# A causal mask added by VectorE where it finds the row maximum, with three smaller moves, in a two-layer hybrid block

## The chip, the cores and the metric

The kernel runs on one core of one Trainium2 chip. The metric is the device time of one execution in microseconds (us); lower is better. Of the kernel before there are three timed runs, 1093.37, 1095.77 and 1095.83 us, with the median 1095.77. A further execution was recorded by the hardware profiler: its own time is 1094.5 us, and the span that the trace covers is 1092.8 us.

## The reference

A block of two layers works on 512 tokens of width 1024 in float32. Each layer mixes tokens, adds the normed result to the residual `h`, and runs a gated feed-forward network of hidden width 2816. Layer 0 mixes by a gate with a spatial matrix per group of 128 columns; layer 1 mixes by attention with a forget gate over 12 heads of 64 columns. Both layers also attend over 256 memory rows with 4 heads. What the change touches is this:

```
# layer 0: spatial gating; w is lower triangular, its rows are summed where ln_b enters
s = einsum('gts,bcsgd->bctgd', tril(w_s), layernorm(gelu(v), ln_g, ln_b)) + b_s
# layer 1: forgetting attention, per head
c = cumsum(log_sigmoid(s_in @ w_f + b_forget))              # the gate sums
logits = q k^T * scale + c[t] - c[s]
logits = where(s <= t, logits, -inf)
o = softmax(logits) @ v
# end of layer 1
h = h + rmsnorm(f, ln_ffn_post[1])                          # the last scale rows are ln_ffn_post[1]
```

## The kernel before

Every float32 product is made of three matmuls: a value is split into a high part (`whi`, a cast by ScalarE, line 276) and a low part (`wlo`, the rest, a subtraction by VectorE, line 277), and `mm3` multiplies high by high, low by high and high by low (lines 219 to 221). So every weight that arrives by DMA passes through ScalarE and VectorE before TensorE can use it. The feed-forward networks use a seven-product scheme for block pairs and take most of the time; the change touches them only at their edges.

A scheduler orders the work: it gives each engine and each DMA queue one fixed list, and a queue runs its list strictly in order. The order of the program text sets the priorities. Pools of buffers hold the scheduler to a number of live tiles: PSUM has three tags, `mm` and `lg` with three tiles each and `tr` with two.

The masked attention of layer 1 is run by `attend` (line 562), one head after the other, in steps. While head n gets its logits, the probabilities of head n-1 are turned and multiplied. `S3`, `S2`, `S1`, `S0` are `FoxHead.logits` (line 530) for blocks of 128 queries; block tb has (tb+1) x 128 keys, so 512, 384, 256 and 128 columns of `lg` in PSUM. `N` steps scale the probabilities `p` by the reciprocal of their sums `sm` (lines 478 and 480). `T` steps turn them by TensorE (line 487) and split the turned tile `tr` into the two parts `pT`; `V` steps multiply by the values (line 556). `F` steps take other work in between: here the value and key projections that are still to be done (`v`, `qk`), and later the first part of the output projection (`y`).

One call of `logits` issues two float32 matmuls for the head (`qa` with `ka`, then `qc` with `kc`, whose rows 64 to 67 carry the gate sums) and a third one in bfloat16, `ident_b` times `neg`, which adds the causal mask to the 128 columns on the diagonal (line 537). Then `weigh` (line 467) finds the negated maximum `nmx` by VectorE from PSUM (line 470), and ScalarE takes the exponent from PSUM into `p` with the sum of each row in `sm` (line 471).

The parts of a head, `qa`, `qc`, `ka` and `kc`, are put together by eight transfers on SP's queue in `head_parts` (lines 1567 to 1578): six copy parts of queries and keys, and two copy gate sums out of `cc`. `cc` is made from the `cs` matmuls (line 1546) by ScalarE and VectorE (lines 1550 to 1553). In the text, the first head's parts come behind `cc`.

The other three places: `spatial_bias` (line 735) sums the rows of the six triangular matrices with `tri`, in 12 matmuls of 128 columns (line 744); `boundary` (line 949) norms the residual between a mix and the product behind it, with `evacuate` called behind the second step (k = 1) of the third group of products, which puts the norm's factors into PSUM as `rb` (line 287) from `r`, a power taken by GpSimd (line 290); and `end_gains` (line 1619) turns the last scale rows into full tiles by eight TensorE transposes into `gr` (line 1625) and two copies by ScalarE (line 1628).

## Time and profile before

| what | value |
|---|---|
| timed runs, median (lowest to highest) | 1095.77 us (1093.37 to 1095.83) |
| the profiled execution, its own time | 1094.5 us |
| its span in the trace | 1092.8 us |
| mean granted TensorE clock | 0.998 |
| TensorE matmul busy | 99% |
| VectorE busy | 86% |
| ScalarE busy | 67% |
| GpSimd busy | 5% |
| mean DMA rate | 164 GB/s |

The difference of 1.7 us between the execution's own time and its span lies around the traced work. A matmul's row in the trace starts when it is taken up and includes the time through the array, so rows of neighbouring matmuls overlap; what one costs is read from the start of one to the start of the next. DVE is VectorE, ACT is ScalarE, POOL is GpSimd, PEld is TensorE's loading of weights, and SPq is SP's queue of DMA issues.

### The profile page before, as it was taken

What the parts mean: (1) busy time and instruction counts of PE and PEld (TensorE: products, weight loads), DVE (VectorE), ACT (ScalarE), POOL (GpSimd) and SP (SyncE); (2) the same over time, 40 slices, a digit from 0 to 9 for tenths busy, and PEclk for the clock granted to TensorE, in tenths of its full rate; (3) what the DMA queues carried; (4) which work ended last, traced back from release to release, by engine and by line L of the source; (5) the groups of instructions that cost most, each with busy time, mean ns of one, the idle gap of its engine ahead of it and who ended that gap; (6) DMA issues with size and microseconds to landing.
All of it is one profiled execution on the core that took longest, in us unless ns stands there. A gap on an engine that the chain in (4) does not pass through costs nothing.

```text
span 1092.8 us, 20047 instructions
## 1 busy us (share of the span) xinstructions
PE 1080.9 (99%) x7286; PEld 982.6 (90%) x7286; DVE 941.6 (86%) x1839; ACT 736.9 (67%) x1609; POOL 59.4 (5%) x74
## 2 busy tenths in 40 slices
PE   9999999999999999999999999999999999999997
PEld 7998889999999888998988888889999999988996
DVE  7889658999989999986987798958999998999975
ACT  8776458766666767567666577758766666667563
POOL 0101010000000000001110000010100000000000
PEclk9999999999999999999999999999999999999999
DMA  7554875867644447267592654535877553546232
GB/s 271 164 160 128 215 174 190 234 196 191 174 136 147 144 126 248 85 210 182 146 268 70 174 124 117 150 97 157 233 224 195 156 157 118 174 132 199 90 115 77
DMA packets 129834, 178.98 MB, mean 164 GB/s; under 512 B 8204, under 2 KB 92184, under 8 KB 129736
## 3 DMA queue, kind: packets, MB, share of 16 engines
q1 hardware_dynamic: 118376, 160.23, 46.8%
q0 software_dynamic: 10944, 17.30, 10.0%
q8 instruction: 57, 0.93, 0.3%
q14 instruction: 41, 0.34, 0.1%
q10 hardware_dynamic: 416, 0.18, 0.1%
HBM read 158.18 MB, written 42.99 MB: 184 GB/s over the span
## 4 chain that ended last, share of the span: by engine, by line
PE 89%; ACT 3%; DMA 3%; DVE 2%; issue 1%; POOL 1%; SPq 0%; POOLq 0%; DVEq 0%; ACTq 0%
PE a L219 7%; PE a L221 7%; PE a L220 7%; PE e L219 3%; PE e L220 3%; PE e L221 3%; PE ps L221 3%; PE ps L220 3%; PE ps L219 3%; PE y L219 3%; PE y L220 3%; PE y L221 3%; PE p L219 3%; PE p L221 3%; PE p L220 3%; PE x L219 3%
## 5 line engine op out<-in xcount | busy, mean ns | idle before, releaser
L277 DVE TENSOR_TENSOR wlo<-raw,whi 128x512 fp32r<-128x512 f32 x316 | 210.8, 685 | 21.4 <-ACT whi L276 18.2
L276 ACT CAST whi<-raw 128x512 fp32r<-128x512 f32 x316 | 189.0, 619 | 56.2 <-PE a L220 14.6
L219 PE MATMUL a<-xshi,whi 128*128 128x256 f32 x480 | 135.3, 282 | 0.0
L220 PE MATMUL a<-xslo,whi 128*128 128x256 f32 x480 | 134.7, 281 | 0.0
L221 PE MATMUL a<-xshi,wlo 128*128 128x256 f32 x480 | 134.5, 280 | 0.0
L276 ACT CAST whi<-room 128x512 fp32r<-128x512 f32 x160 | 98.3, 621 | 47.9 <-PE x L220 9.5
L277 DVE TENSOR_TENSOR wlo<-room,whi 128x512 fp32r<-128x512 f32 x160 | 108.7, 686 | 6.4 <-ACT whi L276 3.8
L219 PEld LDWEIGHTS a<-xshi,whi 128*128 128x128 f32 x480 | 90.4, 188 | 1.9 <-ACT e L1107 1.1
L220 PEld LDWEIGHTS a<-xslo,whi 128*128 128x128 f32 x480 | 90.4, 188 | 0.7
L221 PEld LDWEIGHTS a<-xshi,wlo 128*128 128x128 f32 x480 | 90.5, 188 | 0.0
L221 PE MATMUL ps<-xshi,wlo 128*128 128x256 f32 x192 | 54.3, 285 | 1.0 <-DVE wlo L277 1.0
L220 PE MATMUL ps<-xslo,whi 128*128 128x256 f32 x192 | 53.9, 283 | 0.6 <-DVE xslo L277 0.6
L219 PE MATMUL ps<-xshi,whi 128*128 128x256 f32 x192 | 53.7, 287 | 0.0
L276 ACT CAST ff<-u 128x256 fp32r<-128x256 f32 x80 | 32.3, 406 | 29.3 <-PE p L221 15.4
L219 PE MATMUL y<-whi,mixedhi 128*128 128x512 f32 x128 | 51.6, 403 | 0.0
L220 PE MATMUL y<-wlo,mixedhi 128*128 128x512 f32 x128 | 50.6, 395 | 0.0
L219 PE MATMUL p<-whi,ff 128*128 128x512 f32 x128 | 50.5, 396 | 0.0
L221 PE MATMUL y<-whi,mixedlo 128*128 128x512 f32 x128 | 50.5, 394 | 0.0
L220 PE MATMUL p<-wlo,ff 128*128 128x512 f32 x128 | 50.4, 394 | 0.0
L221 PE MATMUL p<-whi,ff 128*128 128x512 f32 x128 | 50.2, 394 | 0.0
L219 PE MATMUL x<-xshi,whi 128*128 128x256 f32 x160 | 45.0, 281 | 0.0
L220 PE MATMUL x<-xslo,whi 128*128 128x256 f32 x160 | 44.9, 281 | 0.0
(376 smaller groups left out, 3575.3 us busy)
## 6 DMA issues: line engine op xcount, KB each, us to landing
room<-in_w_up SPq DMA_DIRECT2D x36, 512.0 KB
raw<-in_w_gate SPq DMA_DIRECT2D x24, 512.0 KB
raw<-in_w_down SPq DMA_DIRECT2D x20, 512.0 KB
sums<-in_w_gate SPq DMA_DIRECT2D x16, 512.0 KB
sums<-in_w_gate POOLq DMA_DIRECT2D x16, 512.0 KB, 5.8
raw<-in_w_out SPq DMA_DIRECT2D x16, 512.0 KB
sums<-in_w_down SPq DMA_DIRECT2D x32, 256.0 KB
sums<-in_w_down POOLq DMA_DIRECT2D x16, 512.0 KB, 8.1
```

Of the source, the lines that this page charges most:

```text
L219: PE.matmul(o, w[0], x[0], start=start, stop=False, skip_group_check=more)
L220: PE.matmul(o, w[0], x[1], start=False, stop=False, skip_group_check=more)
L221: return PE.matmul(o, w[1], x[0], start=False, stop=stop, skip_group_check=more)
L276: last_hi[0] = A.copy(hi, src)
L277: last_split[0] = last_hi[0], (eng or V).tensor_sub(lo, src, hi)
```

## The change

Four parts move together.

1. The mask matmul is gone, and `ident_b` and `neg` with it. A constant `mask` (128 x 512 in bfloat16: zeros, and the triangle in the last 128 columns) takes their place. VectorE now makes one pass over `lg` that adds the mask, negates, writes the result to `p` in SBUF and keeps the least value, which goes to `nmx` by a second instruction. ScalarE takes the exponent in place, from `p` to `p`.
2. The last scale rows come by transfers: at the start of the program 1024 numbers of `gains` are written to a scratch tensor `row` in DRAM, and later two transfers spread its halves over 128 partitions.
3. `spatial_bias` takes two groups at a time: 6 matmuls of 256 columns.
4. The first head's parts stand ahead of the gate sums; only its two transfers from `cc` stay behind them. In `boundary`, `evacuate` is called one step of k later.

The diff, cut to its core:

```
-    ident_b = cp.tile([P, P], BF16, name="ident_b")
-    V.tensor_copy(ident_b, ident)
...
-    neg = cp.tile([P, P], BF16, name="neg")
-    V.tensor_copy(neg, neg_f[:, :P])
+    mask = cp.tile([P, T], BF16, name="mask")
+    V.tensor_copy(mask[:, : T - P], neg_f[:, P:])
+    V.tensor_copy(mask[:, T - P :], neg_f[:, :P])
...
-            PE.matmul(lg[:, :n], qc[:68, c], kc[:68, :n], start=False, stop=False)
-            PE.matmul(lg[:, c], ident_b, neg, start=False, stop=True)
+            PE.matmul(lg[:, :n], qc[:68, c], kc[:68, :n], start=False, stop=True)
...
-            self.weigh(tb, lg[:, :n], (self.beside if tb == 0 else self.room)[:, at : at + n])
+            p = (self.beside if tb == 0 else self.room)[:, at : at + n]
+            x = slice(tb, tb + 1)
+            V.tensor_tensor_reduce(out=p, in0=lg[:, :n], in1=mask[:, T - n :], scale=-1.0, scalar=3.0e38,
+                                   op0=ALU.add, op1=ALU.min, accum_out=self.nmx[:, x])
+            last_exp[0] = A.activation(p, p, AF.Exp, bias=self.nmx[:, x], scale=-1.0, accum_out=self.sm[:, x])
+            self.p[tb] = p
...
-                for n in range(2):
-                    o = ps("lg", (P, 384), s="rows")
-                    for g in range(3):
-                        for part in range(2):
-                            PE.matmul(o[:, g * P : (g + 1) * P], tri[:, 384:], ws[3 * n + g][:, part, :],
-                                      start=part == 0, stop=part == 1)
+                for n, both in enumerate(two_ws):
+                    o = ps("lg", (P, 2, P), s="rows")
+                    for part in range(2):
+                        PE.matmul(o, tri[:, 384:], both[:, :, part, :], start=part == 0, stop=part == 1)
...
-        outs = group(ws[:2], inputs(1), h0, ["mm", "lg"], after={1: evacuate})
+        outs = group(ws[:2], inputs(1), h0, ["mm", "lg"], after={2: evacuate})
...
+        def head_sums(u, n):
+            _, qc, _, kc = u.parts
+            nc.sync.dma_start(qc[66:68, :].bitcast(F32), cc[n : n + 33 : 32, :].bitcast(F32))
+            nc.sync.dma_start(kc[64:66, :].bitcast(F32), cc[64 + n : 64 + n + 33 : 32, :].bitcast(F32))
...
+            if n:
+                head_sums(u, n)
...
+        for f in before[-1]:
+            f()
         for f in take(fill, 2):
             f()
         cs = ps("mm", s="cs")
...
+        head_sums(heads[0], 0)
         ys, outs = out_part(1, mixed)
         more = queue(outs)
         credit[0] = 0
-        for f in take(fill, 2) + before[-1] + take(fill, 3):
+        for f in take(fill, 5):
...
+        row = dp.tile([KT, P], F32, tag="row", name="row")
+        c = (G_FFN_POST + 1) * KT
+        nc.sync.dma_start(row.rearrange("m c -> c m"), i["gains"][:, c : c + KT])
         for dh in range(2):
-            o = ps("tr", s="gr")
-            for m in range(4):
-                PE.transpose(o[:, m * P : (m + 1) * P],
-                             gain(G_FFN_POST + 1, 4 * dh + m).to_broadcast([P, P]), ident)
             gain_rows.append(plain("gr"))
-            A.copy(gain_rows[dh], o)
+            nc.sync.dma_start(gain_rows[dh], row[4 * dh : 4 * dh + 4, :].rearrange("m c -> (m c)").partition_broadcast(P))
```

How the lists move is shown at three places. First TensorE's list at the second head's first two blocks of logits (`lg` of 512 and 384 columns), with the turning of the first head's probabilities (`tr`) between them. Before:

```order
L535 MATMUL lg_7936<-ka_7829,qa_7828 128x512
L536 MATMUL lg_7936<-kc_7716,qc_7714 128x512
L537 LDWEIGHTS ident_b
L537 MATMUL lg_7936<-neg,ident_b 128x128
L487 MATMUL tr_7951<-ident,p_7862 128x128
L487 MATMUL tr_7951<-ident,p_7842 128x128
L487 MATMUL tr_7951<-ident,p_7825 128x128 x2
L535 MATMUL lg_7960<-ka_7829,qa_7828 128x384
L536 MATMUL lg_7960<-kc_7716,qc_7714 128x384
L537 LDWEIGHTS ident_b
L537 MATMUL lg_7960<-neg,ident_b 128x128
```

Now:

```order
L533 MATMUL lg_7926<-ka_7822,qa_7821 128x512
L534 MATMUL lg_7926<-kc_7657,qc_7655 128x512
L485 MATMUL tr_7940<-ident,p_7853 128x128
L485 MATMUL tr_7940<-ident,p_7834 128x128
L485 MATMUL tr_7940<-ident,p_7818 128x128 x2
L533 MATMUL lg_7949<-ka_7822,qa_7821 128x384
L534 MATMUL lg_7949<-kc_7657,qc_7655 128x384
```

The mask's matmul and its load of weights are gone after each block, and the rest keeps its order here.

VectorE's list at the same blocks (`nmx` is the negated maximum, `pT` the turned probabilities, `vf` values of a projection, `sm` the row sums). Before:

```order
L277 TENSOR_TENSOR pT_7929<-tr_7927,pT_7928 128x512
L470 TENSOR_REDUCE nmx_7723<-lg_7936 128x1
L277 TENSOR_TENSOR pT_7953<-tr_7951,pT_7952 128x512
L470 TENSOR_REDUCE nmx_7723<-lg_7960 128x1
L1500 TENSOR_SCALAR vf_7912<-v_7914,r_4_6412 128x256
L470 TENSOR_REDUCE nmx_7723<-lg_7993 128x1
```

Now:

```order
L275 TENSOR_TENSOR pT_7919<-tr_7917,pT_7918 128x512
L542 ISA p_7929,nmx_7664<-lg_7926,mask 128x512
L542 ISA nmx_7664 128x1
L275 TENSOR_TENSOR pT_7942<-tr_7940,pT_7941 128x512
L542 ISA p_7952,nmx_7664<-lg_7949,mask 128x384
L542 ISA nmx_7664 128x1
L1501 TENSOR_SCALAR vf_7902<-v_7904,r_4_6406 128x256
L542 ISA p_7984,nmx_7664<-lg_7981,mask 128x256
L542 ISA nmx_7664 128x1
```

Each of the 48 reductions has become two instructions: the pass over the block, and one that reads the least value out.

SP's queue at the first head's parts. Before:

```order
L1576 DMA qc_7713<-whi_7759 64x512
L1576 DMA qc_7714<-whi_7759 64x512
L1576 DMA kc_7715<-wlo_7762 64x512
L1576 DMA kc_7716<-wlo_7762 64x512
L1577 DMA qc_7713<-cc 2x512
L1578 DMA kc_7715<-cc 2x512
L1576 DMA qa_7767<-whi_7759 64x512
L1576 DMA qa_7767<-wlo_7760 64x512
L1576 DMA ka_7768<-whi_7761 64x512 x2
```

Now:

```order
L1567 DMA qc_7654<-whi_7686 64x512
L1567 DMA qc_7655<-whi_7686 64x512
L1567 DMA qa_7694<-whi_7686 64x512
L1567 DMA qa_7694<-wlo_7687 64x512
L1567 DMA ka_7695<-whi_7688 64x512 x2
L1567 DMA kc_7656<-wlo_7689 64x512
L1555 DMA qc_7654<-cc 2x512
L1556 DMA kc_7656<-cc 2x512
```

The transfers of `qa` and `ka` now stand ahead of the two that wait for `cc`.

More of the change, by code (lines that the diff above doesn't have):

```diff
@@ L56, in hybrid @@
     n_of = {}
-    last_load, last_exp, last_split, last_hi, last_turn = [None], [None], [None], [None], [None]
+    last_load, last_exp, last_split, last_hi, last_turn = ([None] for _ in range(5))
     def name(s):
@@ L725, in layer_a @@
                             compare_op=ALU.is_ge, fill=0.0, base=0, channel_multiplier=-1)
-            ws = []
+            ws, two_ws = [], []
             def spatial_parts():
@@ L732, in spatial_parts @@
                     split(wsf[:, g * P : (g + 2) * P].rearrange("p (a c) -> p a c", a=2), both[:, :, 0, :], both[:, :, 1, :])
+                    two_ws.append(both)
                     ws.extend(both[:, n] for n in range(2))
@@ L738, in spatial_bias @@
                 V.tensor_copy(vcols, o)
-                for n in range(2):
-                    o = ps("lg", (P, 384), s="rows")
-                    for g in range(3):
-                        for part in range(2):
-                            PE.matmul(o[:, g * P : (g + 1) * P], tri[:, 384:], ws[3 * n + g][:, part, :],
-                                      start=part == 0, stop=part == 1)
-                    for g in range(3):
-                        c = bsp[:, 3 * n + g, :]
-                        V.scalar_tensor_tensor(out=c, in0=o[:, g * P : (g + 1) * P],
-                                               scalar=vcols[:, NG + 3 * n + g : NG + 3 * n + g + 1], in1=c,
+                for n, both in enumerate(two_ws):
+                    o = ps("lg", (P, 2, P), s="rows")
+                    for part in range(2):
+                        PE.matmul(o, tri[:, 384:], both[:, :, part, :], start=part == 0, stop=part == 1)
+                    for g in range(2):
+                        c = bsp[:, 2 * n + g, :]
+                        V.scalar_tensor_tensor(out=c, in0=o[:, g, :],
+                                               scalar=vcols[:, NG + 2 * n + g : NG + 2 * n + g + 1], in1=c,
                                                op0=ALU.mult, op1=ALU.add)
@@ L1539, in layer_b, with pair_split, head_parts, values @@
         attend(mem_heads(1, qm, mixed), between=between)
+        qcs, kcs = [[act(s) for _ in range(2)] for s in ("qc", "kc")]
+        for t in qcs + kcs:
+            G.memset(t[64:68, :].bitcast(F32), 1.0)
+        pair = {}
+        def pair_split(pr):
+            pair["q"], pair["k"] = pair_of_parts(), pair_of_parts()
+            split(qs[pr], *pair["q"])
+            split(keys[pr], *pair["k"])
+        def head_sums(u, n):
+            _, qc, _, kc = u.parts
+            nc.sync.dma_start(qc[66:68, :].bitcast(F32), cc[n : n + 33 : 32, :].bitcast(F32))
+            nc.sync.dma_start(kc[64:66, :].bitcast(F32), cc[64 + n : 64 + n + 33 : 32, :].bitcast(F32))
+        def head_parts(u, n):
+            own, other = rows(u.j)
+            qc, kc = qcs[n % 2], kcs[n % 2]
+            u.parts = qa, qc, ka, kc = act("qa"), qc, act("ka"), kc
+            (qh, ql), (kh, kl) = pair["q"], pair["k"]
+            for dst, src in ((qa[own, :], qh), (qa[other, :], ql), (ka[own, :], kh), (ka[other, :], kh),
+                             (qc[:64, :], qh), (kc[:64, :], kl)):
+                nc.sync.dma_start(dst.bitcast(F32), src[own, :].bitcast(F32))
+            if n:
+                head_sums(u, n)
+        heads, before = [], {}
+        for n in range(HEADS):
+            pr, j = divmod(n, 2)
+            u = FoxHead(pr, j, split_vals[pr % 2], mixed)
+            def values(u=u):
+                for t2 in range(2):
+                    src = vals[u.pr // 2, t2][:, :, (u.pr % 2) * P : (u.pr % 2 + 1) * P]
+                    dst = u.vals[:, 2 * t2 : 2 * t2 + 2]
+                    split(src.rearrange("p a (b c) -> p a b c", b=2), dst[:, :, :, 0, :], dst[:, :, :, 1, :])
+            make = lambda u=u, n=n: head_parts(u, n)
+            before[n - 1] = [make] if j else [lambda pr=pr: pair_split(pr), make, values]
+            heads.append(u)
+        for f in before[-1]:
+            f()
         for f in take(fill, 2):
@@ L1553, in layer_b @@
         V.tensor_sub(nl, ch, cs[:HEADS, :])
-        qcs, kcs = [[act(s) for _ in range(2)] for s in ("qc", "kc")]
-        for t in qcs + kcs:
-            G.memset(t[64:68, :].bitcast(F32), 1.0)
-        pair = {}
-        def pair_split(pr):
-            pair["q"], pair["k"] = pair_of_parts(), pair_of_parts()
-            split(qs[pr], *pair["q"])
-            split(keys[pr], *pair["k"])
-        def head_parts(u, n):
-            own, other = rows(u.j)
-            qc, kc = qcs[n % 2], kcs[n % 2]
-            u.parts = qa, qc, ka, kc = act("qa"), qc, act("ka"), kc
-            (qh, ql), (kh, kl) = pair["q"], pair["k"]
-            for dst, src in ((qa[own, :], qh), (qa[other, :], ql), (ka[own, :], kh), (ka[other, :], kh),
-                             (qc[:64, :], qh), (kc[:64, :], kl)):
-                nc.sync.dma_start(dst.bitcast(F32), src[own, :].bitcast(F32))
-            nc.sync.dma_start(qc[66:68, :].bitcast(F32), cc[n : n + 33 : 32, :].bitcast(F32))
-            nc.sync.dma_start(kc[64:66, :].bitcast(F32), cc[64 + n : 64 + n + 33 : 32, :].bitcast(F32))
-        heads, before = [], {}
-        for n in range(HEADS):
-            pr, j = divmod(n, 2)
-            u = FoxHead(pr, j, split_vals[pr % 2], mixed)
-            def values(u=u):
-                for t2 in range(2):
-                    src = vals[u.pr // 2, t2][:, :, (u.pr % 2) * P : (u.pr % 2 + 1) * P]
-                    dst = u.vals[:, 2 * t2 : 2 * t2 + 2]
-                    split(src.rearrange("p a (b c) -> p a b c", b=2), dst[:, :, :, 0, :], dst[:, :, :, 1, :])
-            make = lambda u=u, n=n: head_parts(u, n)
-            before[n - 1] = [make] if j else [lambda pr=pr: pair_split(pr), make, values]
-            heads.append(u)
+        head_sums(heads[0], 0)
         ys, outs = out_part(1, mixed)
```

## The prediction

> **What bounds the kernel now.** I read the page's first and fourth parts, then what TensorE waits for, then the busy time in stretches of the masked attention (some 607 to 710 us).

> ```profile
> PE 1080.9 (99%) x7286; PEld 982.6 (90%) x7286; DVE 941.6 (86%) x1839; ACT 736.9 (67%) x1609; POOL 59.4 (5%) x74
> PE 89%; ACT 3%; DMA 3%; DVE 2%; issue 1%; POOL 1%; SPq 0%; POOLq 0%; DVEq 0%; ACTq 0%
> PE lg L535 <- DMA ka<-whi: 1.1, 1, 1.1
> ...
> PE rb L287 <- POOL r L290: 0.5, 2, 0.3
> 610.00:710.00 100.00, 99.95 (x639) 85.20 (x638) 91.43 (x216) 73.68 (x189) 0.00 (x0) 1.00 0.55 144
> 620.00:630.00 10.00, 10.00 (x59) 8.31 (x59) 9.22 (x23) 7.10 (x18) 0.00 (x0) 1.00 0.73 233
> 630.00:640.00 10.00, 10.00 (x65) 8.58 (x64) 9.73 (x25) 7.08 (x19) 0.00 (x0) 1.00 0.49 111
> 670.00:680.00 10.00, 9.95 (x58) 7.98 (x58) 9.87 (x26) 8.37 (x25) 0.00 (x0) 1.00 0.72 174
> 680.00:690.00 10.00, 10.00 (x58) 8.12 (x58) 9.70 (x24) 7.77 (x22) 0.00 (x0) 1.00 0.57 147
> 710.00:720.00 10.00, 10.00 (x52) 8.38 (x52) 3.71 (x6) 4.51 (x9) 0.00 (x0) 1.00 0.00 0
> ```

> TensorE is busy for 99% of the span and makes 89% of the chain that ended last, so what it no longer has to do is time won, as long as nobody makes it wait. In the attention it never idles, but VectorE (the third pair of numbers after the stretch) is close behind it: 91.4 of 100 us, and 9.2 to 9.9 of 10 in four stretches. There a saving of TensorE and an addition to VectorE meet. Right after the attention VectorE has 3.7 of 10, so a lag is not carried further.

> **Part 1, the mask on TensorE.** The timeline shows two blocks of a head with their neighbours (start, duration).

> ```profile
> 640.19 0.48 PE L535 MATMUL lg<-ka,qa 128*128 128x512 f32 x1
> 640.51 0.39 PE L536 MATMUL lg<-kc,qc 68*128 68x512 f32 x1
> 640.74 0.23 PE L537 MATMUL lg<-neg,ident_b 128*128 128x128 bf16 x1
> 640.80 0.61 PE L487 MATMUL tr<-ident,p 128*128 128x128 f32 x4
> ...
> 641.43 0.34 PE L536 MATMUL lg<-kc,qc 68*128 68x384 f32 x1
> 641.61 0.23 PE L537 MATMUL lg<-neg,ident_b 128*128 128x128 bf16 x1
> 641.65 0.36 PE L219 MATMUL v<-whi,shi 128*128 128x256 f32 x1
> 641.85 0.28 PE L220 MATMUL v<-wlo,shi 128*128 128x256 f32 x1
> 641.97 0.28 PE L221 MATMUL v<-whi,slo 128*128 128x256 f32 x1
> ```

> From the mask's start to the next start are 0.06 us (640.74 to 640.80) in the first case. In the second it is 0.04 us, and the matmul behind it takes 0.20 us to the next start where a neighbour of its size takes 0.12 (641.85 to 641.97): the mask is too short to cover the next load of weights, which costs 0.08 more. So a mask costs 0.06 to 0.12 us, and 48 of them 2.9 to 5.8 us. I take the middle, 0.09: **-4.3 us**.

> **Part 1, the mask on VectorE.** The groups by shape in the stretch 600 to 715 us (busy us, mean ns):

> ```profile
> L277 DVE TENSOR_TENSOR pT<-tr,pT 128x512 fp32r<-128x512 f32 x24 | 16.1, 683 | 1.6 <-ACT pT L276 1.5
> L470 DVE TENSOR_REDUCE nmx<-lg 128x1 f32<-128x512 f32 x12 | 8.2, 681 | 5.1 <-PE lg L537 5.1
> L478 DVE RECIPROCAL sm<-sm 128x2 f32<-128x2 f32 x24 | 3.8, 160 | 2.3 <-ACT p L471 2.2
> L470 DVE TENSOR_REDUCE nmx<-lg 128x1 f32<-128x128 f32 x12 | 3.4, 282 | 0.0
> L471 ACT ACTIVATION_READ_ACCUMULATOR p<-lg,nmx 128x1 f32 x48 | 9.6, 200 | 0.0
> ```

> The new pass has one source in PSUM and one in SBUF. The nearest row is `pT`, also such a pass: 683 ns for 512 columns, where the reduction takes 681. So I cost the pass itself at what the reduction costs; the trace has no pass of this kind that also reduces. The instruction that reads the least value out is new. Its nearest rows are VectorE's shortest instruction here, 160 ns, and ScalarE's reading of its sum, 200 ns. Bounds: nothing (it runs out while the next instruction starts up) to 0.20 us; I take the middle, 0.10. That is 48 x 0.10 = 4.8 us more for VectorE, 0.48 in each 10 us.

> Where does it decide? TensorE's 10 us become 9.57 in each stretch. In the four full stretches VectorE has 9.22 + 9.73 + 9.87 + 9.70 = 38.5 us, with the addition 40.4, against 4 x 9.57 = 38.3 of TensorE: it lags by 2.1 us. In the other six it has 52.9 + 2.9 = 55.8 against 57.4 and keeps up. So VectorE gives back **+2.1 us**; with the bounds, 0.2 to 5.4. How a lag reaches TensorE, two rows show: the last probabilities are scaled, and the next head's turning starts.

> ```profile
> 681.97 0.54 DVE L480 TENSOR_SCALAR p<-p,sm 128x256 f32<-128x256 f32 x2
> 682.79 0.60 PE L487 MATMUL tr<-ident,p 128*128 128x128 f32 x4
> ```

> Only 0.28 us lie between (682.51 to 682.79); behind that turning, TensorE's whole list is queued. ScalarE reads `p` from SBUF in place of `lg`, at 74% busy without effect; `lg` is free earlier, which no wait of TensorE asks for.

> [...]

> **Part 4, the first head.** TensorE's one long wait of the stage, and SP's issues before it:

> ```profile
> 605.91 0.28 PE L220 MATMUL v<-wlo,shi 128*128 128x256 f32 x1
> 607.27 0.47 PE L535 MATMUL lg<-ka,qa 128*128 128x512 f32 x1 [1.08 <-DMA ka<-whi]
> 599.62 0.58 SPq L1577 DMA_DIRECT2D qc<-cc  x1
> 600.42 0.50 SPq L1578 DMA_DIRECT2D kc<-cc  x1
> 602.25 1.19 SPq L1576 DMA_DIRECT2D ka<-whi  x2
> ...
> L276 ACT CAST whi<-raw 128x512 fp32r<-128x512 f32 x316 | 189.0, 619 | 56.2 <-PE a L220 14.6
> ```

> From 605.91 to 607.27 are 1.36 us where 0.12 would do: 1.24 us lost. The transfers of `qa` and `ka` stood behind the two that waited for `cc`. Now they go out before those; what is late next is `cc` itself: two casts (0.62 us each, the last row) now stand ahead of it on ScalarE's list, so its transfers go out 1.2 us later, near 601 and 602 us, and have 3 us until the first logits, near 605 us without the wait and with nine matmuls moved behind them. I take **-1.2 us**, with 0 (if `cc` lands as late as `ka` did) as the other end. The weights of the third value block are issued later on SP's queue, behind the parts of the second head, but their first matmul is the `v` row of 641.65 above.

> **Part 4, `evacuate`.** TensorE reaches `rb` before GpSimd has `r`:

> ```profile
> 758.96 0.28 PE L220 MATMUL ps<-xslo,whi 128*128 128x256 f32 x1
> 759.49 0.43 PE L287 MATMUL rb<-ident,r 128*128 128x128 f32 x2 [0.25 <-POOL r L290]
> ```

> 0.53 us from start to start, 0.41 more than the usual 0.12. The three matmuls that now come first fill 0.35. It happens in both feed-forward networks (the wait's count of 2): **-0.7 us**; 0 if GpSimd is later too.

> **Parts 2 and 3.**

> ```profile
> L744 PE MATMUL rows<-whi,tri x12: 272/274/327, 75.8 to 77.1; 128*128 128x128 f32 x12
> ...
> 1056.50 0.28 PE L221 MATMUL a<-xshi,wlo 128*128 128x256 f32 x1
> 1056.62 0.60 PE L1625 MATMUL gr<-ident,gains 128*128 128x128 f32 x4
> 1057.23 0.39 PE L219 MATMUL a<-xshi,whi 128*128 128x256 f32 x1
> 1057.45 0.28 PE L220 MATMUL a<-xslo,whi 128*128 128x256 f32 x1
> DMA  9699999999752100000000000001988899888886
> ```

> The twelve sums of rows start over 1.3 us, 0.11 each; six of 256 columns at 0.12 make 0.7: **-0.6 us**. One set of four `gr` transposes costs 0.61 us and 0.10 of delay behind it (1057.23 to 1057.45); I put the second at 0.4, without the wait: **-1.1 us**. What replaces them runs on the DMA engines. The strip is their busy share in tenths from 18 to 34 us in 40 slices: `row` is issued between the loads of memory keys and values and finds them idle from 24 to 29 us; those idle 5 us hide its 1024 pieces. If it took longer than that gap, the memory values' weights would be late by the rest. The two spreads stand ahead of the last three loads of `w_up` and `w_gate` on SP's list, and are used at the very end.

> **Sum.** 1094.5 - 4.3 + 2.1 - 1.2 - 0.7 - 0.6 - 1.1 = **1088.7 us**. The profiled execution stands 1.3 us below the median, inside the three runs; I do not correct for it. A measurement of this kernel tells 0.3%, or 3.3 us, from no change.

> **Rivals.**

> *TensorE alone decides.* VectorE's work has slack to move in, since splits of weights are done before they are needed, and it gives nothing back: 1086.6 us. For it: no row has TensorE waiting for VectorE here. Against: 9.87 and 9.70 of 10 leave no room. Chance 0.15.

> *The read-out costs what ScalarE's costs.* At 0.20 us VectorE gets 9.6 us more: 42.4 against 38.3 in the full stretches, 58.7 against 57.4 in the others, 5.4 us back. That eats the mask's gain; 1094.5 + 1.1 - 3.6 = 1092.0 us, no change that can be told. Chance 0.20.

> *The pass runs at half the rate, and VectorE becomes the bound: slower.* From 282 to 681 ns over 384 columns the reduction takes 1.04 ns a column; a second such for the mean 320 columns is 0.33 us, 16 us in all. VectorE would need 91.4 + 16 + 4.8 = 112.2 us against 95.7: 16.5 back, 1094.5 + 12.2 - 3.6 = 1103.1 us. For it: a pass that adds, scales and reduces at once is not in the trace. Against: `pT`, with two sources, keeps the rate. With all other parts won, the change loses from VectorE at 103.6 us on, that is 0.25 us more per block. [...] Chance 0.14.

> *The moved transfers change nothing for TensorE* (first head and `evacuate` as late as before): 1090.6 us. Chance 0.05, inside the forecast's range.

> **How the numbers follow.** The forecast has 0.46, with its own range of 1086 to 1092. Faster by over 0.3%: nearly all of it, TensorE alone, the moved transfers: 0.60. Within 0.3%: the dear read-out and the forecast's upper edge: 0.21. Slower: the half rate and what a shifted order of the lists may spoil: 0.19. The range 1085.5 to 1100 leaves out less than 2 in 10, most of it at the half rate.

> **What would show it.** Right: 48 mask matmuls less; the pass near 680 ns at 512 columns and the read-out at 60 to 200 ns; VectorE at 96 to 98% of a stretch that is some 2 us shorter, with the first waits of TensorE for VectorE there, before turnings; no wait for `ka` near 606 us; `rb` without wait; an unchanged start. Wrong: a pass of 1 us at 512 columns, TensorE's waits in the attention above 6 us, or new waits for loads near 30 or 1010 us.

## The result, and the profile after

| | before | changed |
|---|---|---|
| median (lowest to highest), same chip | 1094.65 us (1093.37 to 1095.83) | 1088.3 us (1086.87 to 1089.65) |
| ratio to before, 95% interval | | 0.9942 (0.9929 to 0.9955) |
| profiled execution, its own time | 1094.5 us | 1089.65 us |
| its span | 1092.8 us | 1087.9 us |

The change makes the kernel 0.6% faster, and the forecast of 1088.7 us is met. Its steps are another matter: two of them were wrong, and by luck their errors largely cancel. First the page of the changed kernel, its span, busy times and chain:

```profile
span 1087.9 us, 19948 instructions
PE 1077.5 (99%) x7224; PEld 982.0 (90%) x7224; DVE 943.0 (87%) x1887; ACT 737.0 (68%) x1607; POOL 59.4 (5%) x74
PE 89%; ACT 4%; DVE 2%; DMA 2%; issue 1%; POOL 1%; SPq 0%; POOLq 0%; DVEq 0%
```

TensorE still sets the time, with 89% of the chain. It has 62 matmuls less than before (7286), and VectorE 48 instructions more. Of what TensorE waits for in the changed kernel (total us, times, longest):

```profile
...
PE yt L914 <- ACT ya L907: 0.7, 1, 0.7
...
PE yt L914 <- ACT y L907: 0.6, 1, 0.6
...
PE rb L285 <- POOL r L288: 0.2, 1, 0.2
```

The wait for `ka` is gone, `rb` has one wait of 0.2 us left of two, and two waits at turnings of `y` and `ya` have come that the change doesn't touch. The new instructions, by shape, between 600 and 715 us (busy us, mean ns):

The pass takes 685 ns where the reduction took 681, and its read-out 84 ns. These are durations, and VectorE's rows overlap (the pass below ends 0.08 us behind the next start) as TensorE's do (two rows of 0.28 us start 0.12 us apart at 641.85 us of before), so what an instruction costs VectorE is again read from start to start. The timeline has the pass, its read-out and the next instruction, in the changed kernel:

```profile
614.53 0.68 DVE L542 CUSTOM_DVE_ANT_0 p<-lg,mask 128x512 f32<-128x512 f32 x1
615.13 0.08 DVE L542 DVE_READ_ACCUMULATOR2_ANT nmx<- 128x1 f32 x1
615.13 0.69 DVE L275 TENSOR_TENSOR pT<-tr,pT 128x512 fp32r<-128x512 f32 x1
```

The reduction and the next instruction, before:

```profile
615.88 0.68 DVE L470 TENSOR_REDUCE nmx<-lg 128x1 f32<-128x512 f32 x1
616.47 0.68 DVE L277 TENSOR_TENSOR pT<-tr,pT 128x512 fp32r<-128x512 f32 x1
```

The next instruction starts together with the read-out. From the start of the pass to the next start are 0.60 us, where the reduction had 0.59. Over all blocks the medians are 609, 473, 345 and 209 ns for 512, 384, 256 and 128 columns, against 599, 465, 341 and 201 before. So the new work costs VectorE about 0.01 us a block, 0.4 us for all 48, not 4.0.

Two stretches of the attention (after the stretch: matmuls, weight loads, VectorE, ScalarE, each as busy us):

```profile
630.00:640.00 10.00, 9.91 (x62) 8.44 (x61) 9.97 (x29) 6.49 (x17) 0.00 (x0) 1.00 0.81 212
...
690.00:700.00 10.00, 9.90 (x58) 8.40 (x57) 9.79 (x26) 9.50 (x23) 0.00 (x0) 1.00 0.53 164
```

VectorE is busy for 98 to 100% of these two, and TensorE idles for 0.2 us in them.

**Where the time went, by place.** For this I compared the start of each matmul with the start of the same matmul in the profile of before, and took the median shift over stretches of 10 us. The table shows how the shift changes over each part of the program (us; negative is time won). The experiments are described below; e9 is the changed kernel profiled again, e8 and e10 are the changed kernel without the first head's part, and e6 is the kernel before again.

| part of the program | predicted | changed | e9 | e8 | e10 | e6 |
|---|---|---|---|---|---|---|
| up to 60 us | 0 | +0.96 | -0.25 | -0.01 | +0.23 | +1.33 |
| row sums, 60 to 100 us | -0.6 | -0.60 | -0.60 | -0.60 | -0.59 | 0 |
| turning near 157 us | 0 | +0.55 | +0.93 | +0.42 | +0.27 | +0.05 |
| `rb` near 181 us | -0.35 | -0.51 | -0.52 | -0.53 | -0.44 | 0 |
| 500 to 540 us | 0 | -0.04 | -0.52 | -0.61 | -0.24 | -0.39 |
| first head and masks, 590 to 710 us | -3.4 | -4.42 | -4.23 | -4.99 | -5.03 | -0.23 |
| `rb` near 759 us | -0.35 | -0.39 | -0.40 | -0.45 | -0.46 | 0 |
| 770 to 1050 us | 0 | +0.41 | +0.43 | +0.39 | +0.40 | 0 |
| last scale rows | -1.1 | -0.88 | -0.86 | -0.93 | -0.94 | 0 |

What lies between the rows adds less than 0.1 us. Three rows vary from one execution to the next, whatever the change: the start, the turnings near 157 us, and 500 to 540 us. The kernel before moves by 1.3 us at its start between its two profiles, and the changed kernel by 1.2 the other way. So two profiles can't be compared by their spans to better than about 1 us here. A single part can, to 0.1 us in most rows and 0.2 in that of the first head and masks (the changed kernel against e9).

### The profile page after: what moved, and what is told of

Same layout as the page of the kernel before. It is cut to its first block, busy times and chain, and to the rows that moved or that the text cites. A ratio compares the mean times of both kernels' runs of the same rounds, so it can differ in the third digit from the quotient of the medians.

```text
span 1087.9 us, 19948 instructions
## 1 busy us (share of the span) xinstructions
PE 1077.5 (99%) x7224; PEld 982.0 (90%) x7224; DVE 943.0 (87%) x1887; ACT 737.0 (68%) x1607; POOL 59.4 (5%) x74
## 4 chain that ended last, share of the span: by engine, by line
PE 89%; ACT 4%; DVE 2%; DMA 2%; issue 1%; POOL 1%; SPq 0%; POOLq 0%; DVEq 0%
PE a L217 7%; PE a L219 7%; PE a L218 7%; PE e L217 3%; PE e L218 3%; PE e L219 3%; PE ps L219 3%; PE ps L218 3%; PE ps L217 3%; PE y L217 3%; PE y L218 3%; PE y L219 3%; PE p L217 3%; PE p L219 3%; PE p L218 3%; PE x L217 3%
## 5 line engine op out<-in xcount | busy, mean ns | idle before, releaser
L274 ACT CAST whi<-raw 128x512 fp32r<-128x512 f32 x316 | 188.8, 618 | 57.4 <-PE a L218 14.6
L219 PE MATMUL a<-xshi,wlo 128*128 128x256 f32 x480 | 134.6, 281 | 0.0
L219 PEld LDWEIGHTS a<-xshi,wlo 128*128 128x128 f32 x480 | 90.5, 188 | 0.0
L219 PE MATMUL ps<-xshi,wlo 128*128 128x256 f32 x192 | 54.1, 284 | 0.1
L219 PE MATMUL y<-whi,mixedlo 128*128 128x512 f32 x128 | 50.4, 394 | 0.0
L219 PE MATMUL p<-whi,ff 128*128 128x512 f32 x128 | 50.1, 394 | 0.0
L218 PE MATMUL e<-t,whi 128*128 128x256 f32 x160 | 45.0, 281 | 0.0
```

What stands on the lines that cost most here:

```text
L218: PE.matmul(o, w[0], x[1], start=False, stop=False, skip_group_check=more)
L219: return PE.matmul(o, w[1], x[0], start=False, stop=stop, skip_group_check=more)
L274: last_hi[0] = A.copy(hi, src)
```

## The experiments

**e1, the mask alone.**

```
 before, with
-            PE.matmul(lg[:, c], ident_b, neg, start=False, stop=True)
-            self.weigh(tb, lg[:, :n], ...)
+            V.tensor_tensor_reduce(out=p, in0=lg[:, :n], in1=mask[:, T - n :], ..., accum_out=self.nmx[:, x])
+            last_exp[0] = A.activation(p, p, AF.Exp, bias=self.nmx[:, x], scale=-1.0, ...)
```

> Part 1 alone on the kernel before. By the prediction (VectorE gives back a part of TensorE's gain): -4.3 + 2.1 = -2.2 us, with waits of TensorE for VectorE before turnings between 620 and 690 us. By the rival (TensorE alone decides): -4.3 us, no such waits. The wait for ka near 606 us stays in both.

Measured: 1091.59 us against 1095.14, ratio 0.9969 (0.9957 to 0.9981), so 3.5 us won where 2.2 were predicted. From 590 to 710 us the shift is -3.30. TensorE's waits in that stretch:

```profile
PE lg L533 <- DMA ka<-whi: 1.0, 1, 1.0
PE tr L485 <- DVE p L478: 0.4, 1, 0.4
```

There is one wait for VectorE, of 0.4 us before a turning at 614 us, where the prediction gave 2.1 us back between 620 and 690 us. The result lies between the two theories and nearer to "TensorE alone decides".

**e2, the first head's parts alone.**

```
 before, with
+        for f in before[-1]:
+            f()
         for f in take(fill, 2):
             f()
         cs = ps("mm", s="cs")
...
+        head_sums(heads[0], 0)
```

> The first head's parts ahead of the gate sums, alone on the kernel before. Prediction: -1.2 us, the wait of 1.1 us for ka is gone and none takes its place. Rival: the gate sums' transfers are late instead, 0 us, with a wait for qc or kc near 606 us.

Measured: 1095.23 us against 1095.14, ratio 1.0000 (0.9992 to 1.0009). Neither theory is right. The wait for `ka` is gone, and the shift changes by -1.3 us from 600 to 610 us; but by 650 us all of it has been given back. The timeline shows where, TensorE first, then ScalarE and VectorE (start, duration):

```profile
629.96 0.40 PE L535 MATMUL lg<-ka,qa 128*128 128x512 f32 x1
631.07 0.66 PE L487 MATMUL tr<-ident,p 128*128 128x128 f32 x4 [0.71 <-DVE p L480]
...
627.94 0.63 ACT L276 CAST whi<-q 128x512 fp32r<-128x512 f32 x1
628.45 0.63 ACT L276 CAST whi<-k 128x512 fp32r<-128x512 f32 x1
628.97 0.42 ACT L276 CAST vals<-vf 128x256 fp32r<-128x256 f32 x1
629.28 0.38 ACT L471 ACTIVATE p<-lg,nmx 128x128 f32<-128x128 f32 x1
...
629.87 0.69 DVE L277 TENSOR_TENSOR wlo<-q,whi 128x512 fp32r<-128x512 f32 x1
630.47 0.54 DVE L480 TENSOR_SCALAR p<-p,sm 128x256 f32<-128x256 f32 x2
```

TensorE now comes to a turning before its probabilities are scaled. On ScalarE's list the exponent of the last block stands behind three casts, on VectorE's list a split of `q` stands ahead of the scaling, and the turning starts 1.1 us after the matmul ahead of it. The next such place, at 639.64 us, loses another 0.5 us.

The wait for `ka` had not been covering this. In e4, below, that wait is gone as well, with the first head's parts where they were, and the same turning starts 0.23 us behind its neighbour, as it does before (631.38 to 631.61):

```profile
629.82 0.40 PE L221 MATMUL qk<-shi,wlo 128*128 128x512 f32 x1
630.05 0.60 PE L487 MATMUL tr<-ident,p 128*128 128x128 f32 x4
```

There one cast stands right ahead of the last exponent. So it is the order that the moved part gives to ScalarE's and VectorE's lists that takes the gain back.

**e3, the last scale rows alone.**

```
 before, with
-                PE.transpose(o[:, m * P : (m + 1) * P], gain(...).to_broadcast([P, P]), ident)
+        nc.sync.dma_start(row.rearrange("m c -> c m"), i["gains"][:, c : c + KT])
+            nc.sync.dma_start(gain_rows[dh], row[4 * dh : 4 * dh + 4, :]...partition_broadcast(P))
```

> The last scale rows by transfers, alone on the kernel before. Prediction: -1.1 us, all of it behind 1010 us, and the first 62 us as before. Rival: the 1024 pieces of row take their place among the first loads, and the first 62 us get 0.9 us longer, as they are in the changed kernel: about 0 us in all.

Measured: 1093.43 us against 1095.14, ratio 0.9985 (0.9977 to 0.9994). In its profile the first 60 us shift by +0.1 only, and the place of the transposes by -0.87. The rival falls: the 1024 pieces of `row` hold nothing up. The 0.96 us at the start of the changed kernel's profile are variation, as e6 and e9 show directly.

**e4, the row sums in twos and `evacuate` a step later.**

```
 before, with
-                            PE.matmul(o[:, g * P : (g + 1) * P], tri[:, 384:], ws[3 * n + g][:, part, :], ...)
+                        PE.matmul(o, tri[:, 384:], both[:, :, part, :], start=part == 0, stop=part == 1)
...
-        outs = group(ws[:2], inputs(1), h0, ["mm", "lg"], after={1: evacuate})
+        outs = group(ws[:2], inputs(1), h0, ["mm", "lg"], after={2: evacuate})
```

> The row sums in twos and evacuate a step later, alone on the kernel before. Prediction: -0.6 us near 75 us and -0.35 us at each of 181 and 759 us, -1.3 us in all. Rival for evacuate: GpSimd's r comes later by as much, then only the -0.6 us are left. Neither should touch the first 62 us.

Measured: 1092.07 us against 1095.14, ratio 0.9970 (0.9958 to 0.9981): 3.1 us, more than twice the forecast. The row sums give -0.59 and `evacuate` -0.45 and -0.43 in the profile. The rest was not looked for: -1.36 between 590 and 710 us, where this kernel changes nothing. The wait for `ka` is gone without the first head's part. SP's queue and TensorE in the timeline of e4:

```profile
602.01 1.19 SPq L1575 DMA_DIRECT2D ka<-whi  x2
603.28 0.55 SPq L1575 DMA_DIRECT2D qa<-whi  x1
...
605.67 0.28 PE L220 MATMUL v<-wlo,shi 128*128 128x256 f32 x1
605.79 0.40 PE L535 MATMUL lg<-ka,qa 128*128 128x512 f32 x1
```

The same place on SP's queue before:

```profile
603.53 2.16 SPq L1576 DMA_DIRECT2D qa<-whi  x1
```

The issue right behind `ka` takes 2.16 us before and 0.55 in e4. What else ran there shows in the DMA queues (packets, MB, share of the engines' time) of before from 603 to 604 us

```profile
q1 hardware_dynamic: 118, 0.21, 89.9%
q8 instruction: 1, 0.02, 10.9%
```

and of e4 from 606 to 607 us:

```profile
q8 instruction: 1, 0.02, 8.1%
```

One packet of 16 KB on an instruction queue: before, it starts at 603.56 us, when the transfers of `ka` have just been issued; in e4 at 606.55 us, when the logits have begun. The table has all profiles at this place ("behind" means that the load starts after the first logits):

| profile | load starts, takes (us) | matmuls from it to the first logits | both `ka` issued by | logits late by |
|---|---|---|---|---|
| before | 603.56, 1.75 | 20 | 603.44 | 1.24 |
| e6 (before again) | 605.30, 1.36 | 15 | 604.51 | 1.09 |
| e1 | 604.30, 1.65 | 21 | 604.25 | 1.20 |
| e3 | 604.55, 1.37 | 20 | 604.43 | 0.66 |
| e12 | 604.47, 1.69 | 20 | 604.31 | 1.07 |
| e4 | 606.55, 1.30 | behind, by 4 | 603.19 | 0 |
| e8 | 605.47, 1.42 | behind, by 4 | 602.12 | 0 |
| e10 (e8 again) | 606.06, 1.31 | behind, by 4 | 602.68 | 0 |
| changed, e9 | 605.01 and 603.68 | 4 | 598.32 and 596.98 | 0 |

The whole queue on the page of before (packets, MB):

```profile
q8 instruction: 57, 0.93, 0.3%
```

and on that of e12, whose only addition is 48 matmuls with their loads of weights:

```profile
q8 instruction: 58, 0.95, 0.4%
```

One load more. The packets have 16,384 bytes each, and in the profile of before they start 171 to 322 of TensorE's matmuls and loads of weights apart, 256 in the mean (160 to 324, and 256, in the changed kernel). That they carry TensorE's program is a reading of these counts and of the queue's name, not shown. The load keeps near its place in TensorE's list, whatever the time: in all fourteen profiles it starts between the 4021st and the 4040th matmul. In the three with six row sums less ahead of it and the old head it comes behind the first logits, where the five with twelve row sums and the old head have it beside `ka`. How `ka` lands late shows in the packets of before. Up to 604.84 us they start many at a time. Then none starts until 605.30, when the load is about to end (605.31). Four of 2 KB are left of the transfers issued so far, and they go one behind the other until 606.11. The queues from 605.2 to 606.1 us:

```profile
q1 hardware_dynamic: 4, 0.01, 5.9%
```

The other four profiles with the load beside `ka` have the same four late packets, the first of them within 0.02 us of the load's end. So the last packets go only when the load has ended, while all others are done; the logits follow 0.7 to 1.2 us after the last of the four. A kernel that moves the load and nothing else wasn't tried, so that the load holds them up is a reading too. Why six matmuls move it by 24 is open, and so is whether e4 owes its place to the row sums or to `evacuate`, since it has both.

No wait listed here is one of TensorE for the load itself; a transfer beside it that TensorE is about to need came 0.7 to 1.2 us late in five profiles.

**e5, no mask at all.**

```
 changed, with
-            V.tensor_tensor_reduce(out=p, in0=lg[:, :n], in1=mask[:, T - n :], ...)
+            V.reduce_max(out=self.nmx[:, x], in_=lg[:, :n], axis=AX.X, negate=True)
+            last_exp[0] = A.activation(p, lg[:, :n], AF.Exp, bias=self.nmx[:, x], accum_out=self.sm[:, x])
```

> The changed kernel with no causal mask at all on the diagonal blocks (that part of the computation is left out): VectorE reduces as before, ScalarE reads lg, TensorE has no mask. VectorE loses the 4.0 us of read-outs. If VectorE's lag gives back 2.1 us, as predicted: 2.1 us below the changed kernel, about 1086.2 us, and no waits for VectorE between 620 and 700 us. If TensorE alone decides: the same as the changed kernel within 0.5 us. The small waits of its trace say 0.9 us.

Measured: 1088.16 us, ratio to before 0.9934 (0.9919 to 0.9948); the changed kernel has 1088.3 us and 0.9942. So the read-outs cost no more than the 0.1 to 0.2 us between these medians, which can't be told from nothing. From 590 to 710 us the shift is -4.60, against -4.42 and -4.23 for the changed kernel. The same part of the program (from 610 to 710 us of before), in the changed kernel and then in e5:

```profile
608.64:706.00 97.36, 97.17 (x594) 85.08 (x594) 90.29 (x262) 73.26 (x185) 0.00 (x0) 1.00 0.58 153
606.91:704.09 97.18, 97.01 (x594) 85.16 (x594) 89.69 (x216) 71.53 (x185) 0.00 (x0) 1.00 0.58 153
```

VectorE's busy time, in which what overlaps counts once, differs by 0.6 us. So e5 takes almost no work from VectorE. It confirms that the read-out is nearly free; whether VectorE would have had room for 4 us it does not tell.

**e6, the kernel before again** (no edit).

> The kernel before, profiled a second time. If the wait of 1.1 us for ka near 606 us belongs to the kernel's lists, it is there again within 0.2 us. If it hangs on the slow issue that followed on SP's queue (2.16 us where 0.55 is usual; it is missing in e4, where ka was in time), it comes and goes with that issue, and so do the waits of 0.2 to 1.5 us near 157, 509 and 520 us.

Measured: 1095.5 us, ratio 1.0001 (0.9991 to 1.0012). TensorE's waits have this row again:

```profile
PE lg L535 <- DMA ka<-whi: 0.9, 1, 0.9
```

So the wait belongs to the program, and so does the slow issue (1.84 us in this profile). The start came 1.3 us later than in the first profile, and the 500 to 540 us stretch 0.4 us shorter, with no cause in the program: these vary.

**e7 and e11, more work for VectorE.**

```
 changed, with (e7)
+            V.reduce_max(out=extra[:, x], in_=lg[:, :P], axis=AX.X, negate=True)
 and (e11)
+            V.reduce_max(out=extra[:, x], in_=lg[:, : min(n, 2 * P)], axis=AX.X, negate=True)
```

> The changed kernel with one more reduction over 128 columns per block on VectorE (0.28 us, 48 of them, 13.5 us; its result isn't used). By the prediction's sum, VectorE has 91.4 + 4.0 + 13.5 = 108.9 us against TensorE's 95.7 and becomes the bound: about 13 us more than the changed kernel without lag, 1099 us. If VectorE's other work (splits of weights that are needed later) can move out of the way: at most half of it, below 1095 us.

> The changed kernel with one more reduction per block over its first 256 columns on VectorE (128 in the smallest block; 36 of 0.42 us and 12 of 0.28, 18.5 us; its result isn't used). By the prediction's sum (VectorE has no room in the full stretches): 91.4 + 4.0 + 18.5 = 113.9 against 95.7, 18 us more than the changed kernel. By what e7 showed (13.5 us cost 5.3, the first 8.2 fitted in): 18.5 - 8.2 = 10.3 us more, about 1098.5 us, slower than before.

The additions between 598 and 720 us, e7 first:

```profile
L545 DVE TENSOR_REDUCE extra<-lg 128x1 f32<-128x128 f32 x48 | 13.6, 284 | 0.0
```

and e11:

```profile
L545 DVE TENSOR_REDUCE extra<-lg 128x1 f32<-128x256 f32 x36 | 15.0, 417 | 0.0
...
L545 DVE TENSOR_REDUCE extra<-lg 128x1 f32<-128x128 f32 x12 | 3.4, 286 | 0.0
```

Measured: e7 1093.58 us, ratio to before 0.9985 (0.9973 to 0.9997); e11 1096.34 us, ratio 1.0012 (1.0003 to 1.0020). From start to start the addition costs VectorE 0.20 us over 128 columns and 0.34 over 256 (medians), so 9.7 us in e7 and 14.5 in e11, not the 13.6 and 18.4 of the rows. Against 1088.33 us of e9 they cost 5.3 and 8.0 us: 4.4 and 6.5 us fit in. Priced so, the prediction's way of summing gives 5.4 and 10.2 us over the changed kernel (an estimate), right for e7 and too much for e11. What fits in comes in part from work that is due later: by the last logits VectorE has made 18 splits of `raw` weights since the first in e7 and e11, and 21 in the changed kernel and e5. In e7 such a split is then the longest thing that TensorE waits for:

```profile
PE y L219 <- DVE wlo L276: 1.6, 1, 1.6
```

In e11 the waits come as the prediction described them, before turnings:

```profile
PE tr L486 <- DVE p L479: 4.4, 4, 1.8
```

**e8 and e10, everything but the first head's part.**

```
 changed, with
-        for f in before[-1]:
-            f()
...
-        head_sums(heads[0], 0)
...
+        for f in take(fill, 2) + before[-1] + take(fill, 3):
```

> The changed kernel with the first head's parts behind the gate sums again. By the prediction's sum 1.2 us more than the changed kernel, 1089.5 us, with the wait for ka back. If the gain of the earlier parts is taken back by the wait for the probabilities (as in e2), the same as the changed kernel within 0.4 us.

> The kernel of e8 once more (all parts but the first head's). If leaving the head's part out is worth as much as e8 against the changed kernel: 0.5 to 1 us below e9; if it makes no difference, within 0.4 us of it; by the prediction's sum 1.2 us above. If the wait for ka belongs to the lists, it is missing here again; if it varies from one execution to the next, it may be back (1.0 us).

Measured: e8 1087.48 us, ratio 0.9926 (0.9912 to 0.9940); e10 1087.61 us, ratio 0.9933 (0.9920 to 0.9945); on the same chip as e10, e9 has 1088.33 us. The wait for `ka` is missing both times. So the kernel without the first head's part has a median 0.7 to 0.8 us below the changed one, twice, though the intervals overlap. The profiles agree: -5.0 from 590 to 710 us against -4.4 and -4.2. Part of it shows as a wait before a turning, behind the matmuls that start at 639.23 us in the changed kernel and at 637.74 us in e9, 0.25 us each, that e8 and e10 don't have.

**e9, the changed kernel again** (no edit).

> The changed kernel once more, on the same chip as e10, for a direct comparison and a second profile. If the start, the turnings near 157 us and the place near 520 us only vary from one execution to the next, these 0.3 to 1.4 us come out differently from its first profile, and the stretch from 590 to 715 us comes out the same within 0.3 us.

Measured: 1088.33 us, ratio 0.9937 (0.9924 to 0.9949). The stretch from 590 to 710 us came out 0.2 us apart from the first profile, the start 1.2 us.

**e12, the mask twice.**

```
 before, with
             PE.matmul(lg[:, :n], qa[:, c], ka[:, :n], start=True, stop=False)
+            PE.matmul(lg[:, c], ident_b, neg, start=False, stop=False)
```

> The kernel before with a second mask matmul per block, between the two products (the masked logits get twice the large negative number, the result is the same). If a mask costs TensorE 0.06 to 0.12 us, 48 more cost 2.9 to 5.8 us, by the prediction's middle 4.3 us, with VectorE no busier. If masks were hidden behind the loads of weights: under 1.5 us.

Measured: 1101.61 us, ratio 1.0054 (1.0040 to 1.0068). From 590 to 710 us the shift is +4.79, and +4.96 without the wait for `ka`, which is 0.17 shorter than in the first profile of before: 0.10 us a mask, inside the prediction's bounds. The timeline of one block:

```profile
646.30 0.28 PE L535 MATMUL lg<-ka,qa 128*128 128x256 f32 x1
646.41 0.23 PE L536 MATMUL lg<-neg,ident_b 128*128 128x128 bf16 x1
646.45 0.36 PE L537 MATMUL lg<-kc,qc 68*128 68x256 f32 x1
646.66 0.23 PE L538 MATMUL lg<-neg,ident_b 128*128 128x128 bf16 x1
```

The second product takes 0.21 us from its start to the next (646.45 to 646.66), where the first takes 0.11: 0.10 us more behind a mask, the kind of delay (0.08 us) that the prediction read as the next load of weights.

## Why the prediction was right, and where it was not

**Mask off TensorE, -4.3 us.** Right in kind, and about right in size. Twice the mask costs 0.10 us each; taking it away gives, from 590 to 710 us and without the 1.24 us of `ka`, 3.8 us in e8 and e10 and 3.4 in e5, 0.07 to 0.08 each.

**The pass at the price of the reduction, the read-out at 0.10 us.** The pass is right: 685 against 681 ns, and 10 ns or less from start to start. The read-out is wrong, though its row of 84 ns lies near the 0.10: the next instruction starts with it, so it costs about nothing, which was the lower bound. The two rivals with dearer instructions fall by these rows. The 60 ns that the signs give as the read-out's lower end rest on no run; the runs show the row of 84 ns, with 10 ns or less from start to start.

**VectorE gives back +2.1 us.** This step failed, and the read-out's price is the term that was mis-sized: 4.8 us more for VectorE in the sum, 0.4 us measured. With that the same sum gives back 0.4 us, near its own lower end of 0.2, and e5 puts the cost of the read-outs at 0.1 to 0.4 us. That VectorE decides in the full stretches is not what failed: e7 and e11 show that 9.7 us more cost 5.3 and 14.5 cost 8.0. So the rival "TensorE alone decides" was nearly right in what is given back, but not for its reason, that VectorE's work has slack to move in: some of it has (4.4 to 6.5 us), while the changed kernel hardly asks for any. (The sum also counts four full stretches and leaves out 610 to 620 us, with 9.31 of 10; with it the +2.1 would have been +2.4.) The slower rival's price was too high: 16 us more, a little over e11's 14.5, would have cost some 9 us (an estimate from e7 and e11), about 1097 us and not 1103. The point of decision, 0.25 us more per block, holds: it lies between 0.20 us (e7), with the kernel 0.15% below before, and 0.30 us on average (e11), with 0.12% above.

**The first head's part, -1.2 us.** This step failed as well. The wait is gone, but not by this part: without the part it is gone anyway in e4, e8 and e10. Alone the part takes the wait away and loses as much at the next turnings (e2); beside the others it costs 0.7 us. The prediction asked what would be late next and looked at `cc` only; late next was the scaling of `p`, behind casts and a split that the new order puts ahead of it.

**The two errors together.** For the first head and the masks the sum had -4.3 + 2.1 - 1.2 = -3.4 us; measured are -4.4 and -4.2. By the runs it is some -3.6 for the masks, -1.24 for `ka` and +0.7 for the first head's part, about -4.1 (an estimate). That the whole forecast still came out right to a microsecond is luck: VectorE gave back nearly 2 us less than forecast, and against that the masks gave 0.5 to 0.9 us less, the first head's part cost 0.7 us, and 0.4 us went between 770 and 1050 us.

**Row sums, -0.6 us, and `evacuate`, -0.7 us.** The first is met to 0.01 us. The second gives 0.9 us, 0.45 at each place: the wait of 0.41 goes whole, not only the 0.35 that three matmuls cover. That with one of these two a load on the instruction queue also comes later, and `ka` in time, was not foreseen, and it is worth as much as the first head's part was meant to be.

**Scale rows, -1.1 us.** 0.87 to 0.94 in the profiles. The price of the second set was put too high. The transfers cost nothing at the start (+0.1 us up to 60 us in e3, where the kernel before varies by 1.3).

Of the signs named, no wait for `ka` and the durations of pass and read-out came true. VectorE at 96 to 98% of the attention did not: it has 90.29 of 97.36 us, 93%. The waits for VectorE before turnings are there but small (0.25 us), and `rb` keeps one wait of 0.2 us. Left open: 0.4 us that the changed kernel, e5, e8, e9 and e10 lose between 770 and 1050 us, spread thinly, with no wait that could be named; e2, with neither mask nor scale rows changed, loses them too, e1 loses 1.2 us there, and e7 and e11 lose almost nothing.

## What to carry to other kernels

Price an instruction from its start to the next start, on every engine whose rows overlap: the read-out has a row of 84 ns, and with it a block took VectorE 10 ns more at most. And test a full engine by adding work, which here told more than the busy digits. When a piece of work is moved up, look at the lists of all engines that make what comes next, since the moved part may now stand ahead of it. And take the parts of a change one at a time: the part meant for the wait did not pay, and one meant for something else removed it.

## What the runs showed of the hardware

Packets of 16 KB on the queue that the profile names `instruction` took 0.88 to 1.97 us each in the profile of before, and the one near the first logits started between the 4021st and the 4040th matmul in all fourteen profiles. Where it fell beside a transfer that TensorE was about to need, four packets of that transfer went only when the load had ended, and the logits came 0.7 to 1.2 us late. So an edit 500 us earlier mattered, here in the row sums or in `evacuate` (e4).

On VectorE the read-out of an accumulator (84 ns) and the next instruction start together, and a pass that adds a bfloat16 mask from SBUF to float32 in PSUM, negates, writes and keeps the least value takes from start to start what a plain reduction takes, within 10 ns (609 against 599 ns for 512 columns).

ScalarE's exponent over 512 columns takes 725 ns from SBUF, where the kernel before has this row for the same from PSUM:

```profile
L471 ACT ACTIVATE p<-lg,nmx 128x512 f32<-128x512 f32 x12 | 8.3, 690 | 3.4 <-DVE nmx L470 3.4
```

After two long waits (1.5 us up to 667 and 1.8 us up to 684 us) TensorE's granted clock in e11 was 0.50 from 684.8 to 688.2 us; in the row of the stretch it is the number behind the five busy times:

```profile
680.00:690.00 10.00, 7.88 (x35) 6.28 (x35) 9.84 (x25) 5.60 (x13) 0.00 (x0) 0.83 0.55 140
```

The timeline of e11 there:

```profile
687.03 0.63 PE L220 MATMUL y<-whi,mixedlo 128*128 128x512 f32 x1
687.46 0.63 PE L218 MATMUL y<-whi,mixedhi 128*128 128x512 f32 x1
...
688.51 0.40 PE L218 MATMUL y<-whi,mixedhi 128*128 128x512 f32 x1
688.75 0.39 PE L219 MATMUL y<-wlo,mixedhi 128*128 128x512 f32 x1
```

Matmuls of 512 columns start 0.43 us apart there and 0.24 a microsecond later. The mean clock of that execution was 0.997; in that of e7, with a single wait of 1.6 us, it was 0.999. The fall cost some 1.7 us of e11's 8.0 (an estimate, 0.17 of 10 us). It is one case, and that the waits brought it about is a reading, not shown.

The lowest medians are those of the changed kernel with the first head's parts left where they were, 1087.5 and 1087.6 us in e8 and e10; against the changed kernel's 1088.3 the intervals overlap.
